# Query blocks of an attention kernel in reversed order, one out-projection sum, a later per-layer product, and other orders of issue in the first stage

## The chip, the cores and the metric

The kernel runs on one core of a Trainium2 chip. The metric is the device time of one execution in microseconds (us). Engines are named as in the profile: PE is TensorE's matmul, PEld its weight load, DVE is VectorE, ACT is ScalarE, POOL is GpSimd, SP is SyncE, which here only issues DMAs.

## The reference

One layer on 1024 tokens of width 1024, float32. Two mixer groups read the same normalised projection: a chunkwise retention (8 heads) and a sparse attention in which an indexer picks 256 keys for each query.

```python
h = rms_norm(x, norm_mix); proj = h @ w_in            # split into the parts of both groups
ret = head_group_norm(retention(r_q, r_k, r_v), ret_norm) * silu(r_g)
rel = relu(einsum('bthd,bsd->bths', q_idx, k_idx) * idx_scale)
score = where(valid, einsum('bth,bths->bts', w_idx, rel), -inf)
top_val, top_idx = top_k(score, 256)                  # per query, chunk-causal keys
logits = (q_lat . c_kv[top_idx] + q_pe . k_pe[top_idx]) * scale
dsa = (softmax(logits) @ c_kv[top_idx] @ w_uv) * silu(d_g)
x = x + concat([ret, dsa]) @ w_out
gate = sigmoid(rms_norm(x, norm_ple) @ w_ple_gate)
x = x + gate * (p @ w_ple_proj)
return rms_norm(x, norm_final)
```

## The kernel before, in words

Every float32 operand of a large product is split into a high and a low part, and three matmuls (high x high, high x low, low x high) make one product. A weight tile is loaded on SP's queue, its high part is copied by ACT, its low part is subtracted by POOL (`load_w`, `prep_w`). A planner with a simulated timeline puts the instructions of each engine in order; `high_priority(n)` moves a group forward in that order, and `behind(ins, mark)` with `mark(name, ins)` fixes an order of issue without a wait.

First stage. x transposed is loaded and split, the squares of its rows are summed (`acc`). The product with the indexer's and rotary columns goes into PSUM (`P1`, and `PI[0]` in the two `nb` banks). `tables` computes cosine and sine by VectorE steps and ACT's sine: `cosx`, `sinx` for the indexer and the attention's rotary columns, `cosr`, `sinr` for the retention. `rsqrt` makes the row norm `rstd` from the sums, `spread` lays it out over all partitions (`rstd_b`). `evacuate(0)` copies `PI[0]` out, `t_block(12)` computes the indexer's second block into the `ib` banks, `evacuate(1)` copies that out. `rotate` turns `P1`; `put_plain` and the lines behind it store high and low halves to DRAM (`d_iq`, `d_ik`, `d_qs`, `d_kp`), from which `ks` and `qs` are loaded again for the scores. Meanwhile `n_chunk` computes the token-major columns (chunks 2, 3, 0, 1, later 4, 5): for each of eight row tiles 24 matmuls into half of an `nb` bank, an eviction by ACT with `rstd` into the staging buffer `nst` (three buffers of two tiles each), a POOL product, and stores to DRAM on SP's queue. The scores of the first two tiles are ordered behind chunk 3's tile 2.

Search. For query tiles 2 to 7 the indexer's scores are summed on VectorE (L471, L473), and the 256th score is found bit by bit on VectorE (tiles 2, 3, 5; L645) and on ACT (tiles 7, 6, 4; L661). TensorE goes on with projections. `choose` writes the masks (`bias`, L710).

Attention. `prep_v` and `prep_k` make values and keys (`VD`, `KK`, 16 buffers with the tag `kv`). A query block i has tiles 2i and 2i + 1 and sees 2i + 2 key tiles. For each of 8 heads `attend` computes logits (`lg` banks, L941, L942), adds the mask and takes the maximum on VectorE (L943), the exponential on ACT (L947), transposes on TensorE (`tp` bank, L964), splits (L970, L971), and multiplies by the values (`oo` bank, L999, L1000). `end_block` divides and gates. The blocks run in the order 0, 1, 2, 3. Beside blocks 0 and 1 runs the retention, 16 units of states, scores and output (`retention_unit`; banks `rb` and `ra`, two each). `project` transposes a half row tile of the mixed output (`ra`), splits it, multiplies it by four of the eight `w_out` tiles (`rb`, L1103 to L1105) and adds (L1106). The retention half is projected beside block 2 and stored in `d_xa`; the attention half beside block 3, with `d_xa` loaded again, and stored in `d_xb`. `per_layer` computes p @ w_ple_proj for a row tile beside block 3 (L1125 to L1127), ACT copies it (L1128), and it is stored in `d_pp`.

Closing stretch. For each row tile 0 to 7, `tail_in` loads `d_xb` and `d_pp`, takes the row norm, transposes and splits; `tail_out` multiplies by the gate weights (48 matmuls, L1173), takes the tanh, multiplies by the per-layer product, adds, norms and stores.

Of the kernel before, what the change touches and what calls it, by code (L numbers as in the profile page):

```python
# [8 lines left out]
F32 = mybir.dt.float32  # L9
# [144 lines left out]
def _body(ctx, nc, tc, ap, dbg):  # L154
# [10 lines left out]

    def mark(name, ins):
        for x in marks.pop(name, []):
            tc.add_manual_dep(x.ins, ins.ins.name,
                              mybir.DependencyInfo(mybir.DependencyClass.NoSync, mybir.DependencyReason.DATA),
                              reason="order of issue")  # L170
# [38 lines left out]
    d_xa = dram.tile([NT, 128, 1024], F32, name="d_xa")  # L209
    d_pp = dram.tile([NT, 128, 1024], F32, name="d_pp")  # L210
# [117 lines left out]
    def rsqrt(out, ssum, n, w):  # L328
# [3 lines left out]
        V.tensor_scalar(a, ssum, 1.0 / n, EPS, op0=OP.mult, op1=OP.add)  # L332
# [4 lines left out]
        V.tensor_tensor(out=out, in0=y, in1=z, op=OP.mult)  # L337
# [6 lines left out]
    def angles(col, cos_t):  # L344
        V.tensor_scalar(cos_t, posi, cst[:, CV + col:CV + col + 1], None, op0=OP.mult)

    def tables(cos_t, sin_t):
        ang, kk = cos_t, sin_t
        V.tensor_scalar(kk, ang, 1.0 / (2.0 * math.pi), MAGIC, op0=OP.mult, op1=OP.add)
# [3 lines left out]
        V.tensor_scalar(ang, ang, PI_LO, -PI_LO, op0=OP.min, op1=OP.max)  # L353
        A.activation(sin_t, ang, AF.Sin)
        A.activation(cos_t, ang, AF.Sin, scale=0.5)
        A.activation(cos_t, cos_t, AF.Square)
        V.tensor_scalar(cos_t, cos_t, -2.0, 1.0, op0=OP.mult, op1=OP.add)

    with tc.issue_after(squares.ins):
        angles(1, cosx)  # L360
        tables(cosx, sinx)
        angles(0, cosr)

    def spread(dst, col):
        for h in range(2):
            pr = nb("ib")
            for j in range(4):
                T.matmul(pr[:, 128 * j:128 * j + 128], col[:, 4 * h + j:4 * h + j + 1].to_broadcast([128, 128]), ident,
                         start=True, stop=True)
            A.activation(dst[:, 512 * h:512 * h + 512], pr, AF.Copy)  # L370

    def evacuate(b):
        it = wk("it")
        for h in range(2):
            A.activation(it[:, 512 * h:512 * h + 512], PI[b][h], AF.Copy)
        return it
# [11 lines left out]
    it1 = evacuate(1)  # L388
# [13 lines left out]
    def put_plain(b, it):  # L402
# [3 lines left out]
        for n, t in enumerate((hi, lo)):  # L406
            Y.dma_start(d_iq[n, j0:j0 + nj].rearrange("j h t -> (j h) t"), f(t)[:8 * nj])
# [5 lines left out]
    for h in range(2):  # L413
        sl = slice(512 * h, 512 * h + 512)
        ma, mb = rotate(P1[h], cosx, sinx, h)
        V.tensor_tensor(out=xo[:, :, sl], in0=two(ma), in1=two(mb), op=OP.add)
# [16 lines left out]
    tables(cosr, sinr)  # L433
# [46 lines left out]
    def n_chunk(c, func, place=nb):  # L480
        ws = [load_w(ap["w_n"][c, kg], 256) for kg in range(4)]
        for tg in range(2):
            for a in range(4):
# [23 lines left out]
                if c < 4:  # L507
                    for a2 in range(2):
                        dst = d_v[2 * c + a2] if c < 2 else d_g[2 * (c - 2) + a2]
                        Y.dma_start(dst[:, j - 1:j + 1], st.rearrange("p a (g c) -> g p a c", g=2)[a2])  # L510
# [745 lines left out]
```

## Time and profile before

| what | us |
|---|---|
| median of three runs | 816.79 |
| lowest and highest | 816.59, 823.42 |
| the profiled execution | 815.47 |
| its span in the profile | 813.7 |

The span runs from the first to the last instruction that the profiler saw. All numbers of rows are from that one execution. Busy time is the union of an engine's instructions; for PE it contains modelled ends, and successive matmuls overlap, so the time of a series is read from starts, not from durations.

### The profile page before, as it was taken

The page shows a single profiled execution, that of the slowest core. Times are in us where ns is not written, and L with a number is a line of the kernel's source. Part 1 is how long each engine was busy: PE and PEld are TensorE (multiplying, and loading weights), DVE is VectorE, ACT ScalarE, POOL GpSimd, SP SyncE. Part 2 cuts the span into 40 slices and gives each one's busy share as a digit, 9 for nine tenths or more (in the row PEclk, how much of TensorE's full clock was granted, in tenths as well). Part 3 has the DMA queues.
Part 4 walks back from the last instruction along what each step waited for, and adds up shares of the span by engine and source line. Part 5 has one row for each costly group of instructions (what it writes and reads, how often), then busy time and mean ns, then how long its engine had stood idle before and what let it go on. Part 6 is the DMA issues. An engine that isn't in the chain of part 4 may idle for free.

```text
span 813.7 us, 12654 instructions
## 1 busy us (share of the span) xinstructions
PE 755.0 (93%) x4415; PEld 653.5 (80%) x4415; DVE 587.5 (72%) x1270; ACT 476.8 (59%) x1041; POOL 312.5 (38%) x237
## 2 busy tenths in 40 slices
PE   9959499998999998999989888999999999899995
PEld 6858499987887887998788776878888887688885
DVE  5959058999999899999867877655565655644655
ACT  7544057638999599993666565543564544424333
POOL 2916245182765543740036668520261101310110
PEclk9969899998999999999999999999999999999999
DMA  8403733230532332531746565964445546542511
GB/s 317 123 21 109 189 101 96 78 98 27 145 114 79 117 104 89 173 119 52 194 111 189 171 190 162 268 233 149 160 168 191 168 163 218 195 156 78 180 52 52
DMA packets 65439, 113.89 MB, mean 140 GB/s; under 512 B 5888, under 2 KB 32896, under 8 KB 65376
## 3 DMA queue, kind: packets, MB, share of 16 engines
q1 hardware_dynamic: 61760, 106.53, 42.3%
q10 hardware_dynamic: 3616, 6.55, 2.2%
q8 instruction: 35, 0.57, 0.3%
q14 instruction: 28, 0.23, 0.1%
HBM read 75.45 MB, written 37.62 MB: 139 GB/s over the span
## 4 chain that ended last, share of the span: by engine, by line
PE 51%; DVE 31%; DMA 6%; ACT 4%; issue 4%; POOL 2%; SPq 1%; POOLq 0%; DVEq 0%; ACTq 0%
DVE res L645 8%; PE lg L1173 6%; PE rb L1173 5%; PE rb L1103 3%; PE rb L1104 3%; PE rb L1105 3%; DMA qk<-d_f 3%; PE tp L964 3%; DMA twr<-in_w_out 3%; PE nb L491 2%; PE nb L492 2%; PE nb L493 2%; DVE ad L654 2%; DVE sc L473 2%; DVE athr L656 2%
## 5 line engine op out<-in xcount | busy, mean ns | idle before, releaser
L235 POOL TENSOR_TENSOR wlo<-wraw,whi 128x512 fp32r<-128x512 f32 (+1 forms) x58 | 87.9, 1530 | 68.2 <-ACT whi L234 62.2
L661 ACT ACTIVATE ajunk<-key,cthr 128x1024 bf16<-128x1024 int16 (+5 forms) x96 | 95.5, 995 | 15.4 <-DVE key L622 10.5
L491 PE MATMUL nb<-whi,xhi 128*128 128x256 f32 x256 | 76.3, 300 | 22.8 <-ACT nst L495 14.1
L645 DVE TENSOR_SCALAR_CACHE_REDUCE res<-key,athr 128x384 f32<-128x384 int16 (+5 forms) x96 | 75.5, 786 | 2.1
L492 PE MATMUL nb<-wlo,xhi 128*128 128x256 f32 x256 | 75.6, 296 | 0.7 <-POOL wlo L235 0.7
L493 PE MATMUL nb<-whi,xlo 128*128 128x256 f32 x256 | 74.9, 295 | 0.0
L491 PEld LDWEIGHTS nb<-whi,xhi 128*128 128x128 f32 x256 | 52.1, 204 | 24.9 <-ACT nst L495 14.9
L333 POOL TENSOR_TENSOR rs_y<-rs_a,mhalf 128x1 f32<-128x1 f32 (+1 forms) x26 | 28.0, 1080 | 110.0 <-DVE rs_a L332 107.5
L971 DVE TENSOR_TENSOR t<-tp,t 128x512 fp32r<-128x512 f32 (+1 forms) x72 | 45.5, 643 | 29.7 <-ACT t L970 29.4
L947 ACT ACTIVATE lm<-lm,mxv 128x128 f32<-128x128 f32 (+3 forms) x64 | 49.4, 773 | 18.5 <-DVE mxv L946 17.0
L970 ACT ACTIVATE t<-tp 128x512 fp32r<-128x512 f32 (+1 forms) x72 | 38.9, 558 | 31.5 <-PE oo L1000 18.4
L322 PE MATMUL big<-xhi,whi 128*128 128x512 f32 x144 | 56.0, 391 | 0.5 <-DVE mb L399 0.5
L323 PE MATMUL big<-xlo,whi 128*128 128x512 f32 x144 | 56.2, 390 | 0.0
L324 PE MATMUL big<-xhi,wlo 128*128 128x512 f32 x144 | 55.7, 390 | 0.0
L473 DVE SCALAR_TENSOR_TENSOR sc<-rel,wi,sc 128x1024 f32<-128x1024 f32 (+5 forms) x42 | 51.0, 1214 | 4.3 <-ACT rel L469 1.6
L492 PEld LDWEIGHTS nb<-wlo,xhi 128*128 128x128 f32 x256 | 52.2, 204 | 1.9 <-POOL wlo L235 1.3
L493 PEld LDWEIGHTS nb<-whi,xlo 128*128 128x128 f32 x256 | 51.9, 203 | 0.6
L964 PE MATMUL tp<-cst,lm 128*128 128x128 f32 x288 | 46.8, 276 | 2.5 <-DVE t L971 2.0
L234 ACT ACTIVATE whi<-wraw 128x512 fp32r<-128x512 f32 (+1 forms) x58 | 34.9, 609 | 19.5 <-POOL cg L523 5.4
L943 DVE CUSTOM_DVE_ANT_0 lm<-lg,bias 128x512 f32<-128x512 f32 (+2 forms) x64 | 36.7, 585 | 11.9 <-PE tp L964 6.5
L1106 DVE TENSOR_TENSOR xt<-rb,xt 128x512 f32<-128x512 f32 x32 | 21.9, 689 | 30.3 <-PE rb L1105 25.9
L999 PE MATMUL oo<-t,vd 128*128 128x256 f32 (+1 forms) x144 | 38.1, 284 | 3.2 <-ACT t L970 2.9
(497 smaller groups left out, 2424.5 us busy)
## 6 DMA issues: line engine op xcount, KB each, us to landing
wraw<-in_w_t SPq DMA_DIRECT2D x26, 256.0 KB, 2.8
wraw<-in_w_n SPq DMA_DIRECT2D x24, 256.0 KB, 2.7
d_f<-o SPq DMA_DIRECT2D x8, 512.0 KB, 3.2
qk<-d_f SPq DMA_DIRECT2D x8, 512.0 KB, 4.9
ql<-d_qs SPq DMA_DIRECT2D x16, 256.0 KB, 4.5
qh<-d_qs SPq DMA_DIRECT2D x32, 128.0 KB, 4.9
twr<-in_w_out SPq DMA_DIRECT2D x8, 512.0 KB, 6.7
xt<-in_x SPq DMA_DIRECT2D x8, 512.0 KB, 4.3
```

The costliest lines, as they stand in the source:

```text
L235: G.tensor_tensor(out=lo, in0=raw, in1=f(hi), op=OP.subtract)
L322: T.matmul(outs[h], wh, xhi[k][:, sl], start=k == 0, stop=False)
L323: T.matmul(outs[h], wh, xlo[k][:, sl], start=False, stop=False)
L324: last = T.matmul(outs[h], wl, xhi[k][:, sl], start=False, stop=k == 7)
L473: V.scalar_tensor_tensor(dst, rel[:, :w], wi[:, i, h:h + 1], dst, op0=OP.mult, op1=OP.add)
L491: T.matmul(pb[:, a % 2], xhi[k][:, tsl], wh, start=k == 0, stop=False)
L492: T.matmul(pb[:, a % 2], xhi[k][:, tsl], wl, start=False, stop=False)
L493: last = T.matmul(pb[:, a % 2], xlo[k][:, tsl], wh, start=False, stop=k == 7)
L645: V.tensor_scalar(junk, src[:, KS[i]], thr[:, n:n + 1], 0.0, op0=op, op1=OP.add, accum_out=cnt[:, n:n + 1])
L661: A.activation(junk[:, :128 * (i + 1)], src[:, KS[i]], AF.Sign, bias=self.thr[:, n:n + 1], accum_out=cnt[:, n:n + 1])
L964: T.transpose(tp[:, o:o + 128], pt[a][:, ks_], ident)
L1173: T.matmul(po[c.start // 512][:, c.start % 512:c.start % 512 + c.stop - c.start], a, b[:, c], start=k == 0 and m == 0, stop=k == n - 1 and ...
```

## The change

First stage. The first VectorE step of `rsqrt` is put in order behind the last VectorE step of the indexer's table, the retention table's first step (`angles(0, cosr)`) behind that step of `rsqrt`, and the rest of the retention's table behind the last addition of the indexer's rotation (L416). ACT's sine for the indexer is put in order behind the copies of `evacuate(0)`. The spread of `rstd` is put behind chunk 2's tile 0. The first store of the indexer's block is put behind the store of chunk 2's tiles 2 and 3.

Later. PSUM banks are `lg`, `ra`, `oo` and `tp` with two each, throughout; the retention and the projections share `ra`. Keys of heads 0 and 1 are prepared ahead of the values, through `oo` and `tp`. Blocks run in the order 3, 2, 1, 0, the retention beside blocks 3 and 2 with priority 900 instead of 50; `attend` has priority 600 in blocks 3 and 2 and 300 in blocks 1 and 0 now. `project` takes both halves of a row tile and sums over all eight `w_out` tiles in PSUM; it runs for row tiles 6, 7, 4, 5 beside block 1, 2, 3 beside block 0, and 0, 1 behind it, and `d_xa` is gone. The per-layer product is computed in the closing stretch behind a tile's gate product (ahead of it for the last tile), in the `oo` banks, and read from there by VectorE; `d_pp` and ACT's copies are gone. The closing stretch takes the row tiles in the order 6, 7, 4, 5, 2, 3, 0, 1. Weights are placed in buffers as those come free in the new order.

```diff
+    def queue(ins, first):
+        tc.add_manual_dep(ins.ins, first.ins.name,
...
+                          reason="order of issue")
...
     with tc.issue_after(squares.ins):
         angles(1, cosx)
-        tables(cosx, sinx)
-        angles(0, cosr)
+        _, reduced, sine = tables(cosx, sinx)
+        turn = angles(0, cosr)
...
-    rsqrt(rstd, pss[:, :NT], D, NT)
-    spread(rstd_b, rstd)
+    first, scaled = rsqrt(rstd, pss[:, :NT], D, NT)
+    queue(first, reduced)
+    queue(turn, first)
+    spread(rstd_b, rstd, "chunk 2 tile 0")
...
-    it0 = evacuate(0)
+    it0, last = evacuate(0)
+    queue(sine, last)
...
-            Y.dma_start(d_iq[n, j0:j0 + nj].rearrange("j h t -> (j h) t"), f(t)[:8 * nj])
+            st = Y.dma_start(d_iq[n, j0:j0 + nj].rearrange("j h t -> (j h) t"), f(t)[:8 * nj])
+            if b == 0 and n == 0:
+                behind(st, "chunk 2 stored 3")
...
-    tables(cosr, sinr)
+    first, *_ = tables(cosr, sinr)
+    queue(first, turned)
...
-    places = banks(lg=2, rb=2, oo=1, tp=1, ra=2)
+    places = banks(lg=2, ra=2, oo=2, tp=2)
...
-    prep_at = ("lg", "rb", "lg", "rb")
+    prep_at = ("oo", "tp", "oo", "tp")
...
+    prep_k(0)
+    prep_k(1)
     for j in range(NT):
         prep_v(j)
-    for h in range(8):
+    for h in range(2, 8):
         prep_k(h)
...
-        with tc.high_priority((300, 600, 600, 600)[i]):
+        with tc.high_priority((600, 600, 300, 300)[i]):
             attend(i, h)
...
-    for i in range(2):
+    for b in range(2):
         for n in range(8):
-            with tc.high_priority(50):
-                retention_unit(8 * i + n)
-            attend_at(i, n)
+            with tc.high_priority(900):
+                retention_unit(8 * b + n)
+            attend_at(3 - b, n)
...
+    def project(j, part):
+        parts = []
+        for n, tag in enumerate(("og", "x")):
...
+            pt = bank("ra")
...
         for nh in range(2):
             sl = slice(512 * nh, 512 * nh + 512)
-            po = bank("rb")
-            for k in range(4):
...
+            po = bank("ra")
+            for k, (hi, lo) in enumerate(parts):
+                wh, wl = wo[k]
+                T.matmul(po, hi, wh[:, sl], start=k == 0, stop=False)
+                T.matmul(po, hi, wl[:, sl], start=False, stop=False)
+                T.matmul(po, lo, wh[:, sl], start=False, stop=k == 7)
             V.tensor_tensor(out=xt[:, sl], in0=po, in1=xt[:, sl], op=OP.add)
-        Y.dma_start(dst, xt)
...
+        Y.dma_start(d_xb[j], xt)
+
+    order = (6, 7, 4, 5, 2, 3, 0, 1)
...
     for n in range(8):
-        attend_at(2, n)
+        attend_at(1, n)
+        if n % 2:
+            with tc.high_priority(0):
+                project(order[n // 2], None)
...
+    for h in range(8):
+        attend_at(0, h)
         with tc.high_priority(0):
...
+            if h in (3, 6):
+                project(order[4 + h // 6], None)
+    mixed = end_block(0, V)
+    for k in range(5):
+        wg.append(prep_gate(k, kv4))
+    for j in order[6:]:
+        project(j, mixed[:, j % 2])
+    for k in range(5, 8):
+        wg.append(prep_gate(k, r4))
...
+    def per_layer(p2):
+        po = [bank("oo") for nh in range(2)]
+        gemm(po, [p2[:, 0, k] for k in range(2)], [p2[:, 1, k] for k in range(2)], wp,
+             [slice(0, 512), slice(512, 1024)])
+        return po
...
+            gemm(pg, hi, lo, wg, cuts)
+            pp = per_layer(p2)
...
-            V.scalar_tensor_tensor(sq[:, c], sq[:, c], 1.0, pp[:, c], op0=OP.add, op1=OP.mult)
+            V.scalar_tensor_tensor(sq[:, c], sq[:, c], 1.0, pp[c.start // 512][:, c.start % 512:(c.stop - 1) % 512 + 1],
+                                   op0=OP.add, op1=OP.mult)
...
-    ready = tail_in(0)
-    for j in range(NT):
+    ready = tail_in(order[0])
+    for n, j in enumerate(order):
```

## Rows read from the trace of the kernel before

**Rows 1.** This is the page's table of engines (busy time, share of the span, instructions) and the line of its chain of waits that gives the shares by engine.

```profile
PE 755.0 (93%) x4415; PEld 653.5 (80%) x4415; DVE 587.5 (72%) x1270; ACT 476.8 (59%) x1041; POOL 312.5 (38%) x237
...
PE 51%; DVE 31%; DMA 6%; ACT 4%; issue 4%; POOL 2%; SPq 1%; POOLq 0%; DVEq 0%; ACTq 0%
```

**Rows 2.** This is the table by stretches, each row a stretch in us from the span's start, its length, then busy time and (instructions) of PE, PEld, DVE, ACT and POOL, the granted TensorE clock as a share of 2.4 GHz, the DMA share and GB/s; the two stops of the first stage, what follows each, and the search.

```profile
41.60:50.20 8.60, 0.00 (x0) 0.00 (x0) 7.74 (x9) 1.50 (x3) 0.78 (x1) 0.55 0.00 0
...
50.30:56.20 5.90, 5.90 (x27) 5.90 (x28) 1.57 (x6) 5.67 (x7) 2.05 (x2) 0.50 0.18 46
...
89.30:99.20 9.90, 0.00 (x0) 0.00 (x0) 0.00 (x0) 0.47 (x1) 0.00 (x0) 0.72 1.00 239
...
99.20:103.90 4.70, 4.68 (x22) 4.68 (x23) 0.00 (x0) 1.69 (x3) 2.29 (x2) 0.50 0.02 7
...
165.00:380.00 215.00, 207.78 (x1175) 183.32 (x1175) 206.02 (x459) 172.01 (x460) 114.52 (x73) 0.98 0.33 104
```

**Rows 3.** This is the timeline of TensorE in the first stage: start and duration in us, engine, line, operation, out<-in; in brackets the idle time before it and what ended that.

```profile
39.73 1.84 PE L380 MATMUL ib<-ones,acc 128*128 128x1 f32 x16
...
50.29 0.58 PE L491 MATMUL nb<-whi,xhi 128*128 128x256 f32 x1 [8.73 <-ACT it L375]
...
99.22 0.58 PE L491 MATMUL nb<-whi,xhi 128*128 128x256 f32 x1 [9.97 <-ACT nst L495]
...
108.59 1.09 PE L466 MATMUL big<-ks,qs 96*128 96x512 f32 x4
```

**Rows 4.** This is the timeline of VectorE and of ACT in the first stage, same columns: the first and last operation of the two rotation tables, the first and last VectorE step of the row norm, and the two ACT instructions around the first stop.

```profile
34.26 1.78 DVE L345 TENSOR_SCALAR cosx<-posi,cst 128x1024 f32<-128x1024 int32 x1
...
48.58 0.68 DVE L353 TENSOR_SCALAR cosr<-cosr 128x1024 f32<-128x1024 f32 x1
...
49.18 0.15 DVE L332 TENSOR_SCALAR rs_a<-ib 128x8 f32<-128x8 f32 x1
...
51.71 0.17 DVE L337 TENSOR_TENSOR rstd<-rs_y,rs_z 128x8 f32<-128x8 f32 x1
...
48.70 1.06 ACT L354 ACTIVATE sinx<-cosx 128x1024 f32<-128x1024 f32 x1 [11.10 <-DVE cosx L353]
...
49.66 0.58 ACT L375 ACTIVATE it<-nb 128x512 f32<-128x512 f32 x1
```

**Rows 5.** This is the timeline of SP's DMA queue in the first stage, and the ACT eviction that follows.

```profile
67.74 0.33 SPq L407 DMA_DIRECT2D d_iq<-ih  x1
...
93.67 0.63 SPq L454 DMA_DIRECT2D qs<-d_iq  x1
...
94.34 3.37 SPq L510 DMA_DIRECT2D d_g<-nst  x6
...
98.69 0.47 ACT L495 ACTIVATE nst<-nb,rstd 128x256 f32<-128x256 f32 x1 [11.19 <-DMA d_g<-nst]
```

**Rows 6.** This is the timeline of VectorE and GpSimd around the indexer's rotation, and the first score operation.

```profile
71.44 1.22 DVE L416 TENSOR_TENSOR xo<-ma,mb 128x1024 f32<-128x1024 f32 x1
...
74.81 3.42 DVE L416 TENSOR_TENSOR xo<-ma,mb 128x1024 f32<-128x1024 f32 x1
...
110.37 0.75 DVE L471 TENSOR_SCALAR sc<-rel,wi 128x1024 f32<-128x1024 f32 x1 [27.44 <-ACT rel L469]
...
73.83 3.32 POOL L418 TENSOR_TENSOR xs<-xo,xs 128x1024 fp32r<-128x1024 f32 x1
```

**Rows 7.** This is the timeline of VectorE and TensorE at the end of the search: the last mask, and the first attention matmul.

```profile
389.84 0.32 DVE L710 TENSOR_SCALAR bias<-junk 128x640 bf16<-128x640 bf16 x1
...
404.02 0.22 PE L941 MATMUL lg<-kk,qh 128*128 128x128 f32 x1
```

**Rows 8.** This is the table by stretches from the first attention matmul to the closing stretch, columns as in rows 2; the last row is the sum of the time from 404 to 700.

```profile
404.00:512.00 108.00, 93.23 (x700) 82.89 (x699) 80.34 (x250) 68.79 (x159) 69.18 (x69) 1.00 0.59 172
...
512.00:588.00 76.00, 75.11 (x422) 63.39 (x421) 42.69 (x109) 32.30 (x63) 17.23 (x8) 1.00 0.62 191
...
588.00:682.00 94.00, 93.63 (x535) 79.53 (x534) 54.95 (x129) 50.40 (x98) 24.17 (x17) 1.00 0.48 169
...
404.00:700.00 296.00, 275.86 (x1737) 236.54 (x1736) 189.14 (x507) 161.13 (x336) 115.79 (x96) 1.00 0.58 185
```

**Rows 9.** This is groups of VectorE instructions between 404 and 512 us by line: shape and count, then busy us and mean ns of one, then idle time before them; the largest groups of the retention.

```profile
L827 DVE TENSOR_TENSOR qz<-qk,qz 64x512 fp32r<-64x512 f32 x12 | 11.0, 913 | 5.9 <-ACT qz L826 5.7
...
L865 DVE TENSOR_TENSOR s<-rb,mk 128x512 f32<-128x512 f32 x16 | 10.9, 684 | 1.4 <-PE rb L864 1.4
...
L889 DVE TENSOR_REDUCE vs<-sq 128x8 f32<-128x512 f32 x8 | 5.4, 679 | 0.1
...
L841 DVE TENSOR_TENSOR x<-ra,same 128x512 f32<-128x512 f32 (+1 forms) x8 | 5.0, 619 | 2.0 <-PE ra L839 2.0
```

**Rows 10.** This is the page's group of the additions behind the out-projection, and one piece of the chain of waits in order of time (start, us, what): the 48 gate matmuls of one row tile.

```profile
L1106 DVE TENSOR_TENSOR xt<-rb,xt 128x512 f32<-128x512 f32 x32 | 21.9, 689 | 30.3 <-PE rb L1105 25.9
...
730.98 11.13 PE rb L1173 x48
```

**Rows 11.** This is one row of TensorE's timeline ahead of the closing stretch, and two rows of the DMA issues (KB each, median us from issue to landing).

```profile
698.79 0.66 PE L1191 MATMUL tp<-cst,xt 128*128 128x128 f32 x4 [1.54 <-DVE xT L1195]
...
d_xa<-xt SPq DMA_DIRECT2D x8, 512.0 KB, 5.0
...
d_pp<-xt SPq DMA_DIRECT2D x8, 512.0 KB, 2.6
```

More of the change, by code (lines that the diff above doesn't have):

```diff
@@ L336, in rsqrt @@
         V.tensor_scalar(z, z, -0.5, 1.5, op0=OP.mult, op1=OP.add)
-        V.tensor_tensor(out=out, in0=y, in1=z, op=OP.mult)
+        return first, V.tensor_tensor(out=out, in0=y, in1=z, op=OP.mult)
     cosr = rpool.tile([128, S], F32, name="cosr")
@@ L357, in tables, with spread @@
         V.tensor_scalar(cos_t, cos_t, -2.0, 1.0, op0=OP.mult, op1=OP.add)
+        return first, last, sin
     with tc.issue_after(squares.ins):
         angles(1, cosx)
-        tables(cosx, sinx)
-        angles(0, cosr)
-    def spread(dst, col):
+        _, reduced, sine = tables(cosx, sinx)
+        turn = angles(0, cosr)
+    def spread(dst, col, at=None):
         for h in range(2):
@@ L367, in spread @@
             for j in range(4):
-                T.matmul(pr[:, 128 * j:128 * j + 128], col[:, 4 * h + j:4 * h + j + 1].to_broadcast([128, 128]), ident,
-                         start=True, stop=True)
+                m = T.matmul(pr[:, 128 * j:128 * j + 128], col[:, 4 * h + j:4 * h + j + 1].to_broadcast([128, 128]),
+                             ident, start=True, stop=True)
+                if at:
+                    behind(m, at)
             A.activation(dst[:, 512 * h:512 * h + 512], pr, AF.Copy)
@@ L415, in _body @@
         ma, mb = rotate(P1[h], cosx, sinx, h)
-        V.tensor_tensor(out=xo[:, :, sl], in0=two(ma), in1=two(mb), op=OP.add)
+        turned = V.tensor_tensor(out=xo[:, :, sl], in0=two(ma), in1=two(mb), op=OP.add)
         A.activation(xs[0][:, :, sl], xo[:, :, sl], AF.Copy)
@@ L588, in _body @@
     for c in (4, 5):
[L589 removed]
+        n_chunk(c, AF.Silu, lambda: bank(("lg", "ra")[turns["lg"] > turns["ra"]]))
     def small_w(src, name):
@@ L831, in retention_states @@
         n = 4 - hf
-        pk = bank("rb")
+        pk = bank("ra")
         for c in range(n):
@@ L1198, in tail_in, with tail_out @@
                 lo.append(x2[:, 1, 128 * k:128 * k + 128])
-        return xt, sq, r1, pp, hi, lo
-    def tail_out(j, xt, sq, r1, pp, hi, lo):
-        end = j == NT - 1
-        pg = [bank("rb" if j % 2 else "lg") for nh in range(2)]
+        return xt, sq, r1, p2, hi, lo
+    def per_layer(p2):
[3 more added lines that the diff above has]
+        return po
+    def tail_out(j, xt, sq, r1, p2, hi, lo):
+        end = j == order[-1]
+        pg = [bank("ra" if j % 2 == order[-1] % 2 else "lg") for nh in range(2)]
         cuts = [slice(0, 512), slice(512, 1024)]
@@ L1233, in tail_out @@
             eng.dma_start(ap["out"][128 * j:128 * j + 128, c], xt[:, c])
-    ready = tail_in(0)
-    for j in range(NT):
-        after = tail_in(j + 1) if j + 1 < NT else None
+    ready = tail_in(order[0])
+    for n, j in enumerate(order):
+        after = tail_in(order[n + 1]) if n + 1 < NT else None
         tail_out(j, *ready)
```

143 lines of the change are left out of this document (49 added, 94 removed).

## The prediction

> **What bounds the kernel now.** I read the page's engine table first, then the chain that ended last: TensorE is busy 93% of the span and holds 51% of the chain, VectorE 31% [rows 1]. No single engine therefore sets the time; each stage has its own limit, and what can be won is TensorE's idle time plus the time in which it ran at the lower of its two clocks. 755.0 of 813.7 us busy leaves 58.7 us idle. The timeline and the table by stretches place it. In the first stage TensorE stands still twice: 8.6 us from 41.6 on and 9.9 us from 89.3 on; after each stop the granted clock is 0.50, that is 1.2 instead of 2.4 GHz, for 5.9 and 4.7 us [rows 2, 3]. At half clock half of that is lost: 2.95 and 2.35 us. So the first stop costs 11.5 us and the second 12.2. From 165 to 380, the search for the selected keys, TensorE is busy 207.8 and VectorE 206.0 of 215 us: both nearly full, so the stretch keeps its length and moves with its start [rows 2]. From 404 to 700 (attention, retention, out-projection) TensorE lacks 20.1 of 296 us, and 14.8 of these lie between 404 and 512, where the two small query blocks run beside the retention chains [rows 8]. The closing stretch is TensorE alone, 11.13 us for the 48 gate matmuls of a row tile [rows 10].
>
> **First stop.** TensorE has finished the sums of squares at 41.6 and could start chunk 2 of the token-major projection, but both PSUM banks for it still hold the indexer's block. ACT, which works in order, stands at the sine of the indexer's table until VectorE has written it at 48.6, and only then, at 49.66, copies the bank out [rows 3, 4]. VectorE computes two tables interleaved, 14 operations from 34.26 to 49.26 [rows 4]. The change puts the sine behind the copies, so a bank is free about 0.6 us after 39.7, before TensorE asks for it. It also keeps the second table out: 7 operations instead of 14 are 7.5 us instead of 15.0, so the norm's first step stands at about 42 instead of 49.18, and rstd, 2.5 us behind it, at about 44.5 instead of 51.71. The spread of rstd over the partitions is ordered behind chunk 2's first tile. A tile is 24 matmuls at half of 5.90/27, 0.109 us, so 2.6 us [rows 2]: it ends at 44.2, and a stall there would be a few tenths. Bounds for this part: 11.5 gained if nothing waits, 0 if the copies stay behind; I take 10.5, near the upper end, because 49.66 is named as the release and nothing else stands between. What is pushed back is the second table (7 operations, two more on rstd_b, its sines, and a second switch of ACT's function table). It now starts after the indexer's rotation, ordered there. VectorE afterwards idles 27.44 us before the first score operation at 110.37 [rows 6], which covers the 9 to 10 us; if the cover were gone, the full 10 us would stand in front of the scores.
>
> **Second stop.** Chunk 2's tiles 6 and 7 need one of three staging buffers; the stores that free them sit in SP's queue behind all scattered stores and loads of the indexer: SP issues these from 67.74 to 94.3, then six chunk stores at once, and ACT's next eviction comes at 98.69 [rows 5]. The change puts the first indexer store behind the store of chunk 2's fourth tile. Two buffers are then returned early. On SP everything after that store waits with it: the lower halves, the rotated keys and queries, weights for chunk 3, the reloads for the scores. TensorE reaches the fourth tile at 41.6 + 4 x 2.6 + 2 for the spread, 54, or, if the indexer's second block (48 matmuls, 11.1 us by [rows 10]) goes first, 65; eviction and GpSimd's product add some 3. So that store is issued between 57 and 68, against 67.74 now: at worst nothing lost, at best 10 us earlier. Upper bound of the gain 12.2, lower bound 0; I take 8, since the scores also need the reloads and I let these cost 4. First stage: 18.5 us, scores starting near 90 instead of 108.59.
>
> **Prep and start of attention.** Keys for heads 0 and 1 are prepared ahead of the values, in banks attention doesn't use. Before, the first attention matmul comes at 404.02; the first block needed no selection mask. Now block 3 comes first and needs the masks of the last tiles, chosen by 389.84 [rows 7]. The masks are there 14 us before the place where attention starts now, so I count nothing; the 14 us are also the point from which it would cost something.
>
> **Reversed blocks.** The work is the same, its partners change. From 588 to 682 seven heads of block 3 ran with six half projections (24 matmuls at 0.232 plus 4 transposes, 6.0 us) and eight per-layer products (12 matmuls, 2.8 us): 93.6 - 36.0 - 22.4 leaves 35.2, 5.0 us of TensorE a head. From 512 to 588, 75.1 less 8 x 6.0 less one head of block 3 leaves 22.1 for five heads of block 2, 4.4 us [rows 8, 10]. VectorE pays 3 x 0.69 for a half projection, so 54.95 less 12.4 less 3 for scaling gate weights gives 5.6 us a head in block 3, and 42.7 - 16.6 - 5.6 = 20.5, 4.1 us, in block 2 [rows 8, 10]. Blocks 0 and 1 hold 3 and 7 key tiles against 11, so by the same rate 1.2 and 2.8 us a head. Retention's TensorE work is then 93.2 - 32 - 13 (three heads of block 2) = 48 us; on VectorE its four largest groups are 32.3 us [rows 9], with the norm's small steps some 40. Blocks 3 and 2 with retention come to 40 + 35 + 48 = 123 us of TensorE and 45 + 33 + 40 = 118 of VectorE. Both engines would be over 90% used. The 14.8 us of gaps were waits of retention for loads and splits; a head of 5 us fills such gaps better than one of 1.2, but VectorE now has hardly any slack. I expect 123 us of work to take about 132. Behind it blocks 1 and 0 with the projections are TensorE's alone. Bounds: 14.8 won if no gap is left there, and the other side if VectorE stays at its present share, 80.3 in 108: 118 us would then take 159, 27 more than I count, 20 more than now. I take 7, half of the gaps, since VectorE's share in the search, 96%, shows that it can run dense.
>
> **Single sums.** One sum over eight weight tiles replaces two over four: 48 matmuls either way, so nothing on TensorE. Half of 32 additions at 0.689 us disappear from VectorE, 11 us, and eight stores and eight loads of 512 KB [rows 10, 11]; they lay beside TensorE work, so zero, and worth up to 2 if VectorE is the limit there.
>
> **Late per-layer product.** 8 x 2.8 = 22.4 us leave the stretch before 700 and join the closing one, with its loads and splits. TensorE is full in both, so zero; if block 3's or 0's stretch isn't full, the move loses what had filled it. Between 682 and 700 the gaps are 20.1 - 14.8 - 0.9 - 0.4 = 4 us [rows 8], the longest 1.54 [rows 11]; they came from the last attention head, and now the retention half of the last projections can run there. I take 1.5 gained.
>
> **The sum.** 18.5 + 7 + 1.5 = 27. The profiled execution took 815.47 us, 1.8 outside its span and 1.3 under the median 816.79. 815.5 - 27 = 788.5; with 1.3 added, 790.
>
> **Rivals.**
> First, the second table gets in the way. It runs on VectorE while GpSimd splits weights and halves. The same addition took 1.22 us at 71.44 and 3.42 at 74.81, beside a GpSimd product [rows 6]. Nine operations stretched like that are 20 to 25 us, and where they stand ahead of the last rotated halves, the reloads come 10 us later. Then only the first stop is won: 10.5 + 7 + 1.5 = 19, 798. For it: GpSimd has more to do in that stretch than before. Against: 27 us of cover. Chance 0.17. The Trainium skill, GPSIMD Engine Reference, section Key points, says that GpSimd shares its SBUF interfaces with VectorE and that they contend when VectorE has two SBUF inputs; by it the moved table, mostly such operations, is dearer where it goes than where it was. The two additions above agree.
>
> Second, VectorE becomes the limit of blocks 3 and 2. At 83% instead of 96%, 118 us take 142, 10 more than counted: 800. At the present 74% it would be 817. For it: 118 us beside 123, in chains in which each waits for the other. Against: 206 of 215 us in the search. Chance 0.20. Both rivals together, 808: 0.05.
>
> Third, slower: retention through one pair of PSUM banks. States, scores and output of a unit, which had two pairs, now alternate on two banks that later serve the projections too, and out-projection weights wait for the last unit. Now 16 units take 108 us, 6.75 each [rows 8]. Blocks 3 and 2 cover 8 us a unit. It decides when a unit exceeds (132 + 27)/16 = 9.9 us; at 11, 176 us stand against 132, and the time is 834. Against: two units turn the banks five times, and emptying a bank takes VectorE 0.62 to 0.68 us [rows 9]. Chance 0.05.
>
> Fourth, the orders don't do what they say: the planner still lets the copies wait, or puts other work first. Without the first stage 8.5 is left: 808. Chance 0.08.
>
> **How the numbers follow.** Forecast, 778 to 796: 0.45; rivals 0.17, 0.20, 0.05, 0.05, 0.08. The likeliest gives 790. 776 takes in the upper bounds of both stops (5 us) and of the gaps (8 us); 808 takes in the rivals but the slow one. A measurement of this kernel can tell about 1% from no change, 8.2 us: below 808.6 is faster. Faster 0.87, same 0.08, slower 0.05.
>
> **What would show it.** TensorE's timeline without a stop at 41.6, granted clock 1.00 from 41 to 100, the first score near 90, the search ending some 18 us earlier, gaps between attention's start and the closing stretch near 12 us instead of 20, and 14 us a tile at the end. Wrong would be: a score start after 98, a VectorE share over 95% beside an idle TensorE in blocks 3 and 2, or first gate matmuls waiting for weights.

## The result, and the profile after

The changed kernel takes 807.01 us (median of 4 runs, 804.96 to 812.53) against 819.44 us of the kernel before on the same chip (816.59 to 823.42): ratio 0.9864, 95% interval 0.9824 to 0.9903. By the ratio that is 11 us, 1.4%, by the two medians 12.4, where 27 us had been forecast. The time lies above the forecast's 778 to 796 and just inside its outermost bound, 808. A second measurement gave 805.97 against 817.21, ratio 0.9843 (0.9790 to 0.9895). The profiled execution took 805.41 us with a span of 803.6, 10.1 less than the span before.

The page's engine table and chain of after, against [rows 1]:

```profile
PE 754.4 (94%) x4415; PEld 656.1 (82%) x4415; DVE 582.0 (72%) x1254; ACT 469.4 (58%) x1025; POOL 311.9 (39%) x237
PE 53%; DVE 20%; issue 11%; DMA 7%; POOL 4%; ACT 3%; SPq 2%; POOLq 0%; ACTq 0%; DVEq 0%
```

TensorE's idle time fell from 58.7 to 49.2 us and its busy time by 0.6 us. Nearly all of that came from the first stage, whose stops up to the scores add up to 10.1 us instead of 19.3. TensorE's timeline of after shows the waits there (start, duration, in brackets the idle time before and what ended it), against [rows 3]:

```profile
41.79 0.36 PE L502 MATMUL nb<-whi,xhi 128*128 128x256 f32 x1
...
49.39 2.02 PE L371 MATMUL ib<-cst,rstd 128*128 128x128 f32 x16 [1.61 <-issue]
...
84.78 0.58 PE L502 MATMUL nb<-whi,xhi 128*128 128x256 f32 x1 [5.08 <-ACT nst L506]
...
96.71 1.17 PE L477 MATMUL big<-ks,qs 96*128 96x512 f32 x4 [3.20 <-DMA qs<-d_iq]
```

The first stop is gone: chunk 2 starts at 41.79 without a wait. The second has split into one of 5.08 us in front of a chunk matmul and one of 3.20 us in front of the first score. The scores start at 96.71 instead of 108.59, 11.9 us earlier and not 18.5. The same stretch on ACT names the first of the two:

```profile
77.47 0.47 ACT L506 ACTIVATE nst<-nb,rstd 128x256 f32<-128x256 f32 x1 [5.45 <-PE nb L504]
83.31 1.06 ACT L356 ACTIVATE sinr<-cosr 128x1024 f32<-128x1024 f32 x1 [5.36 <-DVE cosr L355]
84.27 0.46 ACT L506 ACTIVATE nst<-nb,rstd 128x256 f32<-128x256 f32 x1
```

ACT stood 5.36 us at the sine of the second table, and the copy that frees chunk 2's bank stood behind it: the first stop's mechanism, moved with the table. VectorE and SP's queue name the second, against [rows 5, 6]:

```profile
69.99 2.89 DVE L351 TENSOR_SCALAR sinr<-cosr 128x1024 f32<-128x1024 f32 x1
...
72.92 1.67 DVE L352 TENSOR_SCALAR sinr<-sinr 128x1024 f32<-128x1024 f32 x1
74.51 3.42 DVE L428 TENSOR_TENSOR xs<-xo,xs 128x1024 fp32r<-128x1024 f32 x1
```

```profile
86.97 0.94 SPq L521 DMA_DIRECT2D d_g<-nst  x2
87.95 0.49 SPq L415 DMA_DIRECT2D d_iq<-ih  x1
...
91.24 0.56 SPq L464 DMA_DIRECT2D qs<-d_iq  x1
```

Two steps of the second table, 4.6 us, went ahead of the last rotated half's lower part (L428), on which SP's scattered stores wait. ACT had that half's upper part ready at 71.17, so L428, started at 74.51, was held up by 3.3 us. And the first indexer store, held behind the store of chunk 2's fourth tile, came at 87.95, because the planner put that chunk store behind everything else; the reload of the queries could only follow.

The middle, in the table by stretches (length, busy time of TensorE, weight loads, VectorE, ACT and GpSimd, granted clock, DMA), against [rows 8]. Attention starts 24 us earlier here, so the first line holds block 3 and retention:

```profile
375.00:512.00 137.00, 126.08 (x859) 111.92 (x860) 114.78 (x282) 88.43 (x165) 66.71 (x65) 0.96 0.47 135
512.00:640.80 128.80, 120.55 (x740) 104.77 (x739) 72.89 (x224) 65.73 (x157) 28.76 (x18) 0.99 0.50 156
```

TensorE lacks 10.9 and 8.25 us there, against 20.1 from 404 to 700 before: the gaps of attention were not won. VectorE is busy 84% of the first stretch. The last mask and the first attention matmul of after, against [rows 7]:

```profile
373.89 0.33 DVE L722 TENSOR_SCALAR bias<-junk 128x640 bf16<-128x640 bf16 x1
379.88 0.39 PE L956 MATMUL lg<-kk,qh 128*128 128x512 f32 x1
```

The masks are done 16 us earlier and attention starts 24 us earlier, as the keys of heads 2 to 7 are now prepared beside block 3 and not ahead of it; the span ends only 10 us earlier.

### The profile page after: what moved, and what is told of

Its sections match the earlier page's. It is cut to its first block, busy times and chain, and to the rows that moved or that the text cites. A ratio compares the mean times of both kernels' runs of the same rounds, so it can differ in the third digit from the quotient of the medians.

```text
span 803.6 us, 12584 instructions
## 1 busy us (share of the span) xinstructions
PE 754.4 (94%) x4415; PEld 656.1 (82%) x4415; DVE 582.0 (72%) x1254; ACT 469.4 (58%) x1025; POOL 311.9 (39%) x237
## 2 busy tenths in 40 slices
DMA packets 60831, 97.11 MB, mean 121 GB/s; under 512 B 5376, under 2 KB 32384, under 8 KB 60768
## 4 chain that ended last, share of the span: by engine, by line
PE 53%; DVE 20%; issue 11%; DMA 7%; POOL 4%; ACT 3%; SPq 2%; POOLq 0%; ACTq 0%; DVEq 0%
PE lg L1165 6%; PE ra L1165 5%; PE big L326 3%; PE big L325 3%; PE big L324 3%; PE oo L1165 3%; DVE res L657 3%; PE nb L502 2%; PE nb L503 2%; PE nb L504 2%; DMA qk<-d_f 2%; PE ra L1122 2%; PE ra L1123 2%; PE ra L1124 2%; DVE sc L484 2%
## 5 line engine op out<-in xcount | busy, mean ns | idle before, releaser
L673 ACT ACTIVATE ajunk<-key,cthr 128x1024 bf16<-128x1024 int16 (+5 forms) x96 | 95.5, 994 | 14.8 <-DVE key L634 10.5
L335 POOL TENSOR_TENSOR rs_y<-rs_a,mhalf 128x1 f32<-128x1 f32 (+1 forms) x26 | 26.2, 1006 | 101.5 <-DVE rs_a L334 98.7
L962 ACT ACTIVATE lm<-lm,mxv 128x896 f32<-128x896 f32 (+3 forms) x64 | 49.5, 775 | 25.6 <-DVE mxv L961 25.4
L1014 PE MATMUL oo<-t,vd 128*128 128x256 f32 (+1 forms) x144 | 40.5, 293 | 7.7 <-ACT os L1017 6.2
L1219 DVE SCALAR_TENSOR_TENSOR sqx<-sqx,oo 128x512 f32<-128x512 f32 (+1 forms) x17 | 10.5, 653 | 49.6 <-PE oo L1165 35.0
```

Of the source, the lines that this page charges most:

```text
L673: A.activation(junk[:, :128 * (i + 1)], src[:, KS[i]], AF.Sign, bias=self.thr[:, n:n + 1], accum_out=cnt[:, n:n + 1])
L962: A.activation(lm[:, :w], lm[:, :w], AF.Exp, bias=mx, scale=0.125, accum_out=den[:, a, h:h + 1])
```

## The experiments

**The first stage alone.** The edits of the diff up to the marks of the stores, in the kernel before.

> The kernel before with the edits of the first stage alone (the sine behind the copies, the norm's step ahead of the second table, the spread behind chunk 2's first tile, the second table behind the rotated halves, the indexer's store behind chunk 2's fourth tile). Blocks 0 to 3, the two half sums and the early per-layer product stay. Theory A: the whole gain of the change comes from here; the scores start near 97 as in the changed kernel, 12 us before the kernel before, and the time is 11 to 13 us under it, as good as the whole change. Theory B, the prediction's: 18.5 us for this stage, scores near 90. Theory C: the later edits brought part of the 11 us; then this kernel gains 6 us or less.

```
+    queue(first, reduced)
+    queue(turn, first)
...
+    queue(sine, last)
...
+    queue(first, turned)
```

807.69 us against 817.19 (0.9886, 0.9826 to 0.9946): 9.5 us. Scores at 96.32. Theory A is the nearest, a little short of its 11 us.

**The later part alone.** The other edits.

> The kernel before with the later edits alone (blocks 3 to 0, the new banks, single sums, late per-layer product); the first stage is as before, scores near 108.6. Theory A: the gaps of attention only change place, so the time is within 3 us of the kernel before. Theory B, the prediction's steps: 7 + 1.5 = 8.5 us faster. Theory C: reversed blocks and banks cost time that the first stage hides in the whole change; then it is 3 to 8 us slower.

```
-    start_block(0)
+    start_block(3)
...
-            with tc.high_priority(50):
-                retention_unit(8 * i + n)
...
+            with tc.high_priority(900):
+                retention_unit(8 * b + n)
```

816.28 us against 817.19 (0.9989, 0.9968 to 1.001): nothing. Theory A. With the run above, the whole gain lies, within the noise, in the first stage, and the prediction's 8.5 us of the later part are missing in a kernel that has no other edit.

**The store's order away**, in the changed kernel.

> The changed kernel without the order that holds the first indexer store behind the store of chunk 2's fourth tile. Theory A: the order pays in staging buffers returned early and costs in reloads issued late (87.95 for that store, 91.24 for the first reload); without it the reload can be issued near 87 and land near 92, but the chunk stores come in a heap behind it, and chunk 2's tiles 6 and 7 wait for a buffer until about 95: scores near 100, 2 to 5 us slower than the changed kernel. Theory B: the order only delays the reload; scores near 92.5, 4 us faster than the changed kernel.

```
-            if b == 0 and n == 0:
-                behind(st, "chunk 2 stored 3")
```

805.51 us (0.9843, 0.9779 to 0.9906), not to be told from the changed kernel by time. The trace decides:

```profile
84.41 0.58 PE L500 MATMUL nb<-whi,xhi 128*128 128x256 f32 x1 [5.08 <-ACT nst L504]
94.21 1.09 PE L475 MATMUL big<-ks,qs 96*128 96x512 f32 x4
```

```profile
68.65 1.20 SPq L519 DMA_DIRECT2D d_g<-nst  x2
...
86.45 0.56 SPq L462 DMA_DIRECT2D qs<-d_iq  x1
```

The stop at the sine is the same, the scores start 2.5 us earlier and without a wait; the first reload is issued at 86.45 instead of 91.24. The order gave nothing here and cost the scores 2.5 us. Theory A fell: no heap of stores stopped TensorE. SP's queue shows why. With the first stop gone chunk 2's first two tiles are done so early that their store goes out at 68.65, ahead of most of the scattered stores, where before the first six chunk stores came behind them all, at 94.34 [rows 5]. A staging buffer is free in time without any order.

**The second table late**, in the changed kernel.

> The changed kernel with two more orders: the second table's first step on VectorE behind the last rotated half's lower part (L428), and its sine on ACT behind the copy of chunk 2's last tile. Theory A: the second table took 4.4 us of VectorE ahead of that lower part and held ACT in front of an eviction until 83.3; both gone, the indexer's stores and reloads come 4 us earlier, TensorE's 5.1 us stop at 80 goes, scores near 92, 4 to 5 us faster than the changed kernel. Theory B: the reload is set by SP's queue and by the order behind chunk 2's fourth tile; then the stop goes but the scores stay near 96, and the gain is under 1 us.

```
-    queue(first, turned)
+    queue(first, rest)
+    behind(sine, "chunk 2 copied 7")
```

808.51 us (0.99, 0.9859 to 0.994), not faster than the changed kernel. The first stage did what theory A said (the 5.08 us stop gone, one of 2.35 at another place, scores at 94.02), but TensorE's waits in the search have a new line:

```profile
PE big L324 <- ACT cthr L679: 4.0, 1, 4.0
```

The last mask:

```profile
376.68 0.33 DVE L723 TENSOR_SCALAR bias<-junk 128x640 bf16<-128x640 bf16 x1
```

A projection matmul's wait of 4.0 us is put down to ACT's threshold step of the search. From the first score to the last mask it took 282.7 us, against 277.2 and 278.9 in two profiles of the changed kernel: the gain was given back in the search. That the new wait is the reason is argued from one profile, not tested.

**Both causes away, chunk 2's stores early.**

> The changed kernel with the second table put late (its first step behind the last rotated half's lower part, its sine behind the copy of chunk 2's last tile), the indexer's store no longer held behind chunk 2's fourth tile, and chunk 2's stores given a higher priority instead, so that SP issues the store of the third and fourth tile ahead of the second rotated half and that of the fifth and sixth ahead of the reloads. Theory A: both causes of the second stop are gone, the sine in front of the eviction and the reload behind the store; TensorE works through to the scores, which start at 89 to 91, where the prediction had them, and the time is 4 to 7 us under the changed kernel's. Theory B: SP's scattered stores, some 9 us of issue from 78 on, set the reload by themselves; then scores near 94 and 2 to 3 us.

```
-                behind(st, "chunk 2 stored 3")
...
+    queue(first, rest)
+    behind(sine, "chunk 2 copied 7")
...
+                        with tc.high_priority(400 if c == 2 else 0):
```

803.57 us against 819.68 (0.9796, 0.9757 to 0.9835). TensorE's timeline:

```profile
91.08 1.19 PE L476 MATMUL big<-ks,qs 96*128 96x512 f32 x2 [4.66 <-DMA qs<-d_iq]
```

Scores at 91.08, 17.5 us earlier than before, where the prediction had put them. What is left is the landing of the reload, 4.66 us, behind SP's scattered stores. The time gives 16 us against the kernel before; against the changed kernel it is 2.4 us by the median on the same chip and 4 to 6 by the ratios, where theory A had 4 to 7. The run has three edits at once; whether the early stores were needed beside the other two was not tried.

**The kernel before, once more.**

> The kernel before itself, once more. In the profile of before TensorE ran at full clock from 404 to 700; in the profiles of the changed kernel and of the two halves of the change, each with gaps of 22 to 23 us there, it fell to half clock in four or five places, 7 to 9 us in all. Theory A: such drops come and go from one execution to the next with the same gaps; then this profile has some of them too, between 2 and 9 us lost. Theory B: the changed programs bring them; then this profile has none, under 2 us.

818.52 us, span 816.7. The table by stretches, to be laid beside [rows 8]:

```profile
404.00:512.00 108.00, 92.64 (x662) 83.55 (x663) 75.44 (x233) 64.05 (x150) 67.11 (x67) 0.94 0.53 159
404.00:700.00 296.00, 277.35 (x1705) 240.75 (x1706) 183.54 (x490) 158.23 (x330) 115.09 (x96) 0.97 0.56 181
```

```profile
401.24 0.22 PE L941 MATMUL lg<-kk,qh 128*128 128x128 f32 x1
```

Theory A. Same program, about the same gaps, but a granted clock of 0.94 and 0.97 where the first profile had 1.00. 3% of 296 us are 9 us of full clock. The span is 3.0 us longer, but attention began 2.8 us earlier (401.24 against 404.02), so from there to the end this execution took 5.8 us more: some two thirds of the lost clock show in the time. The falls of the clock that the profile of after shows (0.96 in its first stretch) need therefore be no effect of the change.

**The weights' copies late**, in the changed kernel, for the longest stop of the middle. ACT and TensorE there:

```profile
516.52 1.06 ACT L1064 ACTIVATE wo3h<-twr 128x1024 fp32r<-128x1024 f32 x1 [2.89 <-DMA twr<-in_w_out]
```

```profile
518.39 0.58 PE L1014 MATMUL oo<-t,vd 128*128 128x256 f32 x1 [3.22 <-ACT os L1017]
```

ACT waits for an out-projection weight with a head's copies queued behind it.

> The changed kernel with one order more: ACT's copies of the out-projection weights 3 to 7 stand behind the copies of block 2's third, fourth and fifth head, so that ACT doesn't wait for a weight with attention's copies behind it. Theory A: the 3.2 us stop of TensorE at 515, the waits around it and the fall to half clock behind it go, and the time is 3 to 6 us lower. Theory B: the first projection then starts later and TensorE lacks filler in block 2; within 1 us of the changed kernel.

```
         wo.append(prep_wo(k, r4 if k < 4 else s4 if k < 7 else kv4))
+        if k > 2:
+            queue(split_w[-1], copied[2, (k + 3) // 2])
```

805.97 us (0.9822, 0.9790 to 0.9854), within what separates two measurements of the changed kernel. TensorE's timeline has the stop a few us further on:

```profile
523.07 1.12 PE L1113 MATMUL ra<-cst,mr 128*128 128x128 f32 x4 [3.35 <-DMA mr<-d_mix]
```

Another stop of the same length took its place. The stop that looked dearest was worth nothing by itself.

**Retention at its old priority**, in the changed kernel.

> The changed kernel with the retention units at the priority that they had before, 50 instead of 900, below that of the attention heads. At 900 all 16 units ran beside block 3's eight heads and ended at 508, block 2's heads followed alone. Theory A: at 50 retention spreads over blocks 3 and 2, as the prediction had assumed, the gaps of 14 us from 380 to 520 halve, and the time is 4 to 7 us lower. Theory B: the gaps are waits in chains and come along; retention ends after 530, the projections start later, and the time is the same within 2 us or up to 10 us longer.

```
-            with tc.high_priority(900):
+            with tc.high_priority(50):
                 retention_unit(8 * b + n)
```

798.51 us against 819.68 (0.9732, 0.9695 to 0.9768): 21 us. That is 7.5 us under the changed kernel's median on the same chip (805.97), and 9 to 11 by the ratios. VectorE's sum of block 2's last head, first of the changed kernel, then of this one:

```profile
568.99 0.42 DVE L1021 TENSOR_REDUCE od<-oo 128x128 f32<-128x256 f32 x1 [1.04 <-PE oo L1020]
```

```profile
557.94 0.41 DVE L1021 TENSOR_REDUCE od<-oo 128x128 f32<-128x256 f32 x1
```

And SP's last store of a retention result, again of the changed kernel and of this one:

```profile
511.71 0.69 SPq L910 DMA_DIRECT2D d_mix<-og  x1
```

```profile
523.97 0.38 SPq L910 DMA_DIRECT2D d_mix<-og  x1
```

Retention ends 12 us later and block 2's heads 11 us earlier. The second of these is in the main another order of the projections. One of the three matmul lines of the projection (L1122), from the first attention matmul to that sum, in the changed kernel and in this one:

```profile
379.88:568.99 189.11, 14.23 (x36) 6.77 (x36) 0.97 0.48 142
```

```profile
378.80:557.94 179.14, 8.19 (x20) 3.76 (x20) 0.97 0.49 143
```

Three times 16 matmuls less, a whole row tile, some 11 us by [rows 10], stand ahead of the heads. Theory A by the time, or a little more; its picture of halved gaps is not what the trace shows, since the idle time of TensorE stays at 49.5 us and its busy time falls to 748.9, partly by a higher clock. How the priority acts on the time is open in this run.

**The later part alone, at 50.**

> The kernel before with the later edits alone, as in the run that gave 0.9 us, but with the retention units at their old priority of 50. Theory A: the reversed blocks are worth what the prediction put on the later part, 8.5 us, and the raise to 900 took it away: 7 to 10 us under the kernel before. Theory B: what 50 brought the whole change came from how it fell in with the first stage; then within 3 us of the kernel before.

```
-            with tc.high_priority(900):
+            with tc.high_priority(50):
                 retention_unit(8 * b + n)
```

806.93 us against 817.21 (0.9862, 0.9783 to 0.9940): 10.3 us, theory A. TensorE's waits from 380 to 700 (total, count, longest), first at 900, then at 50:

```profile
PE oo L1000 <- ACT os L1003: 6.6, 4, 3.5
PE lg L942 <- DVE mxv L944: 4.1, 5, 1.7
PE ra L1095 <- DVE xt L1111: 2.1, 2, 1.7
```

```profile
PE oo L1000 <- ACT os L1003: 3.2, 4, 1.5
PE lg L942 <- DVE mxv L944: 1.8, 5, 0.6
```

More than half of the first line is one wait, at 900:

```profile
527.08 1.06 ACT L1050 ACTIVATE wo3h<-twr 128x1024 fp32r<-128x1024 f32 x1 [3.21 <-DMA twr<-in_w_out]
```

```profile
528.94 0.58 PE L1000 MATMUL oo<-t,vd 128*128 128x256 f32 x1 [3.55 <-ACT os L1003]
```

That is the stop at the out-projection weight again, whose removal gained nothing in the changed kernel. Without it the waits for the output copy are the same, 3.1 and 3.2 us, and the maximum of the scores alone is waited for 2.3 us less. The span fell from 812.8 to 804.1, and 7.7 of these 8.7 us are idle time of TensorE (60.2 and 52.5); no single wait of the table carries it. That the heads' chains are served better when retention fills behind them fits this, but is argued.

**The raise alone, in the kernel before.**

> The kernel before with one number changed: the retention units at priority 900 instead of 50, everything else as before (blocks 0 to 3, old banks, half sums). Theory A: the raise costs by itself, because retention runs dense wherever it stands and its waits fall on fewer heads; 5 to 10 us slower than the kernel before. Theory B: it costs only with block 3 first; beside blocks 0 and 1, whose heads are short, retention is the longest work anyway; within 3 us of the kernel before, and the interaction of both edits is the cause.

```
-            with tc.high_priority(50):
+            with tc.high_priority(900):
                 retention_unit(8 * i + n)
```

813.0 us against 817.59 (0.9938, 0.9906 to 0.9970): 4.6 us faster. Theory A fell, and theory B's 3 us were a little short on the other side. In the old order, beside the short heads of blocks 0 and 1, retention may go first; in the kernel with the later edits it may not. The loss comes from the raise together with another of the later edits. The reversed order, with block 3's long heads, is the likely one; the single pair of retention banks and the changed priorities of the heads were not tried apart from it.

**The changed kernel beside the last runs.**

> The changed kernel itself, beside the next three on the same chip. 10 to 12 us under the kernel before, as at first; the stops of the first stage at the same places, the falls of the clock between 375 and 690 at other ones, since in two profiles of the kernel before they lost 0 and 10 us.

805.97 us; scores at 96.47, stops of 1.7, 5.1 and 2.5 us, the clock between 375 and 690 low at partly other places.

**Both repairs.**

> The changed kernel with the second table late and chunk 2's stores early, and with retention at 50. Theory A: the two effects lie in different stages and add up: 3 to 5 us from the first stage, 8 to 11 from the second, so 13 to 16 us under the changed kernel and 24 to 27 under the kernel before, where the prediction had the change (790). Theory B: a part is lost between them, as late scores and early search are made up at the prep; 18 to 21 us under the kernel before.

```
+    behind(sine, "chunk 2 copied 7")
...
+                        with tc.high_priority(400 if c == 2 else 0):
...
-            with tc.high_priority(900):
+            with tc.high_priority(50):
                 retention_unit(8 * b + n)
```

793.66 us against 817.21 (0.9687, 0.9635 to 0.9739): 23.6 us, 12 under the changed kernel; this version beats both kernels. It falls between the theories, close to A. Scores at 92.10, after a wait of 5.06 us for the reload.

**More work ahead of the reload.**

> As the run before it, with the first two score tiles held behind chunk 3's fifth tile instead of its third, so that TensorE has two more tiles, 5 us, to do while the reload lands (it stood 4.7 us for it, scores at 91.1). Theory A: the scores start at 92 without a stop and at full clock, and 2 to 4 us are won. Theory B: VectorE and ACT set the search, their start moves by 1 us, and the time is the same within 1.5 us.

```
-                        behind(m, "chunk 3 tile 2")
+                        behind(m, "chunk 3 tile 4")
```

810.43 us (0.9906, 0.9874 to 0.9937), 17 us slower than without it; both theories missed. The stop for the reload went, one of 2.34 us came in front of a chunk matmul, and the clock stayed at 1.00 until the scores, but they started at 98.49 and not at 92. The last mask, first of the run before, then of this one:

```profile
371.07 0.33 DVE L722 TENSOR_SCALAR bias<-junk 128x640 bf16<-128x640 bf16 x1
```

```profile
393.22 0.31 DVE L722 TENSOR_SCALAR bias<-junk 128x640 bf16<-128x640 bf16 x1
```

So the loss lies in the search: from the first score to the last mask 294.7 us instead of 279.0, on top of the 6.4 us of later start. What made the search longer wasn't traced.

## Why the prediction went wrong, step by step

**First stop, 10.5 us: right.** The copies go first, the stop is gone. 1.61 us remain in front of the spread: the text gave the first table 7.5 us of VectorE, and it took from 34.59 to 45.13, so rstd came at 49.13 instead of 44.5. That was a mis-sized duration without much price. A step of the table took 1.66 us beside GpSimd's splits of weights and 0.69 alone:

```profile
36.40 1.66 DVE L351 TENSOR_SCALAR sinx<-cosx 128x1024 f32<-128x1024 f32 x1
...
44.52 0.69 DVE L355 TENSOR_SCALAR cosx<-cosx 128x1024 f32<-128x1024 f32 x1
```

**Second stop, 8 us: the step that failed first.** The scores start 11.9 us earlier, so after the first stop little more than 1 us was left. The text read the cause as staging buffers held by late stores and took the order on the indexer's store for the cure. The reading was right for the kernel before, but the earlier start of chunk 2 returned the first buffer already; removing the order brought the scores 2.5 us forward, so it was a cost. And the text let VectorE's 27 us of idle time cover the second table, but the table also has a sine, and ACT works in order: it took the evictions behind it along. The text had named this mechanism for the first stop and did not ask it again of the place to which the table went.

**The first rival** was half right: the second table did get in the way, in front of L428 as it says and in two operations, not nine. With table and store both repaired the scores stood at 91.1, so the forecast's 18.5 us of earlier scores were there to be had, as 17.5; the time gave 16.

**Prep, 0; banks; VectorE as the limit.** The masks were in time. VectorE's share beside block 3 was 84%, as the second rival has it (83%), and not the 89% of the forecast (118 us in 132). That VectorE set the pace isn't shown: TensorE's waits there are for copies of ACT as well. The rival with one pair of banks as the limit didn't appear: retention ended at 511.71, some 8 us a unit.

**Reversed blocks, 7 us, and the end of attention, 1.5 us: the step that failed most.** The text added blocks 3 and 2 and all of retention, 123 us of TensorE, as if they ran mixed. It put no price on the raise from 50 to 900, which is in the diff: a term left at nothing without a reason. At 900 the units went beside block 3, whose last head was summed at 498.93 (the last retention store is at 511.71), and block 2 was left without retention as filler; the later part gained 0.9 us, nothing that can be told from noise. The same edits with 50 brought 10.3 us where 8.5 were forecast; the raise alone, without the later edits, cost nothing and gained 4.6. So the failed term is the raise in the new order. That it costs by taking the filler away is argued.

That 10.3 is close to 8.5 is partly luck. Its interval reaches from 5 to 18 us. At 50 the first attention matmul and block 2's last sum stand here:

```profile
390.93 0.47 PE L942 MATMUL lg<-kk,qh 128*128 128x512 f32 x1 [0.89 <-DMA qh<-d_qs]
```

```profile
565.31 0.42 DVE L1007 TENSOR_REDUCE od<-oo 128x128 f32<-128x256 f32 x1 [2.59 <-PE oo L1006]
```

These are 174 us. Less some 30 us of projections and of keys and values prepared in between (an estimate from the count of their matmuls) about 145 are left, where 132 were forecast. The text's picture of a dense mixed stretch did not come even at 50, and retention ended there, too, well before block 2 (532.5). One of its readings was off as well: it gave three heads of block 2 to the time before 512, but in the kernel before the first of these heads is summed only behind it:

```profile
514.83 0.42 DVE L1006 TENSOR_REDUCE od<-oo 128x128 f32<-128x256 f32 x1
```

**Single sums and the late per-layer product, 0: not tried alone.** VectorE's total fell by 5.5 us and the bytes moved from 113.89 to 97.11 MB; whatever both are worth is inside the 10.3 us of the later part at 50.

**The sum.** 18.5 + 8.5 = 27 was forecast; the version with both repairs gains 23.6. The working found the places; it failed on which instructions queue behind the moved ones, and on one number of the diff. That the measured 807 stands beside the 808 of two rivals is chance: the fourth has the first stage lost and the later part paid, and it was the other way round; the other is the sum of the first two, of which the first came true by half and the second isn't shown.

## What to carry to other kernels

An order of issue that frees one engine moves the waiting instruction to a new place on the others: list what stands behind it there, on each in-order engine and DMA queue, before counting the gain. The rank of work meant as filler is a term of the sum: above the long heads it cost 8 to 10 us here, above the short ones it gained 4.6, so try both. A named stop is not a price: the 3.2 us stop at the weights was removed without a gain, while one priority that shows in no single wait was worth 8 to 10 us.

## What the hardware showed

**Tiny VectorE steps that wait for a whole GpSimd instruction.** The norm's steps on 128x8 elements take 0.15 to 0.17 us alone. In the changed kernel, VectorE's and GpSimd's timelines:

```profile
435.95 1.18 DVE L336 TENSOR_TENSOR rs_z<-rs_y 128x8 f32<-128x8 f32 x1
481.83 2.00 DVE L337 TENSOR_TENSOR rs_z<-rs_z,rs_a 128x8 f32<-128x8 f32 x1
```

```profile
435.82 1.29 POOL L837 TENSOR_TENSOR kk<-qk,kk 128x512 fp32r<-128x512 f32 x1
481.45 2.36 POOL L1065 TENSOR_TENSOR wo0l<-twr,wo0h 128x1024 fp32r<-128x1024 f32 x1 [0.83 <-ACT wo0h L1064]
```

The VectorE steps end at 437.13 and 483.83, the GpSimd instructions beside them at 437.11 and 483.81. The Trainium skill, SBUF — State Buffer, section SBUF: two separate sides, says that the two engines share a pair of ports under an exclusive lock, held for a whole instruction, when the VectorE instruction has two inputs in SBUF and the GpSimd one reads there; these rows agree. By the totals of three lines of the norm (L336 to L338 here) 24 such steps cost 10 to 12 us in the attention stage of the runs at 900 with the later edits and 6 to 8 at 50. That they are part of the raise's price is argued, not shown.

**The clock.** The same program, with 20.1 and 18.7 us of gaps, ran the attention stage at 1.00 in one execution and at 0.97 in another, so a granted clock read from one profile is no property of the kernel. The Trainium skill, TensorE: Matmul & The Clock Gate, section A second HAM failure mode: psum-queue depth-cycling, tells of a clock that goes back and forth when TensorE idles briefly between groups of matmuls; this stretch has such gaps in both executions, and only one of them fell. Why is open.
